# Attention's product of probabilities with values in full float32, each head on its own 64 columns of the array

## The chip, the cores and the metric

The kernel runs on one core of one Trainium2 chip. The metric is the device time of one execution in microseconds; times of several executions are given by their median. Its engines are TensorE (PE; the loading of a stationary operand is shown as PEld), VectorE (DVE), ScalarE (ACT), GpSimd (POOL) and SyncE (SP).

## The reference

A trunk of two layers on x of shape 1 x 256 x 1024, all in float32. Layer 0 is FFN, mLSTM mixer, FFN; layer 1 is FFN, windowed attention, FFN. After each of the six stages x becomes LayerNorm(alpha * x + stage(x)). The stage that the change touches is the attention of layer 1: 16 query heads of size 64, 4 key and value heads (four query heads share one), 256 tokens, a window of 128 to both sides, an ALiBi bias and a sink logit per head.

```python
s = jnp.einsum('bnqkgd,bnskd->bnkgqs', q, kw).astype(jnp.float32) * (HEAD_DIM ** -0.5)
s = jnp.where(valid, s - slopes * dist, MASK_VALUE)
m = jnp.maximum(jnp.max(s, axis=-1, keepdims=True), sink_l)
pe = jnp.exp(s - m)
attn = pe / (jnp.sum(pe, axis=-1, keepdims=True) + jnp.exp(sink_l - m))
o = jnp.einsum('bnkgqs,bnskd->bnqkgd', attn, vw.astype(jnp.float32)).reshape(B, S, nq)
return o.astype(x.dtype) @ w_out
```

The change is about the last einsum, attention's probabilities times values.

## The kernel before

**Products in three terms.** Nearly all products run on operands of type float32r, split in two: a high part (a copy by ACT into float32r) and a low part (the original minus the high part, by DVE). `mm3` (L617) issues three matmuls, high by high, high by low and low by high. The weights, 206 MB of reads over the execution, are loaded by SP and POOL queues into `w_raw` and `s_raw` buffers, split on ACT (`w_hi`) and DVE (`w_lo`) in `high` and `low` of the class `Weights`, and multiplied.

**Order of the work.** Each engine works through its instructions in the order in which the program issues them. The class `Paced` wraps the engines and keeps a clock for each; `on_tensor` (L162) adds a cost for every matmul. In the FFN stages `W.fill` reads these clocks after every matmul and decides which split comes next on ACT and DVE. In the attention stage there is no filler (L1600): `W.done` issues a counted number of splits, from the lists at the head of the file (`PU` for the attention loop), whatever the clocks say.

**The attention stage** (`attn`, L1335). `proj` multiplies x with the columns for keys and values and for the first queries. Its evacuation for m = 0 splits the values into `va[t]`, one tile per block of 128 tokens, of shape 128 x 4 x 5 x 64: for each of the four value heads there are five slots of 64 columns, of which slots 1 and 3 hold the high and the low part and slots 0, 2 and 4 are zeros, filled by POOL (L1371). A window of 128 columns that starts at slot 0 or 1 has the values in its right or left half and zeros in the other half.

Then a loop over `st` from 0 to 10 (L1552) treats heads in eight pairs j, software-pipelined: at step st it does, in this order,

- `values(st - 3)` and the evacuation of its sum into `qT` (high on ACT, low on DVE; rows `q_hi<-pw`, `q_lo<-pw`);
- the rest of the softmax of pair st - 1: `es` on ACT, the sum and its reciprocal `sm` and four scalings of `sc` on POOL (`scale`);
- some of the filling work in `fill[st]`: `q_rest` (remaining query columns) in early steps, `out_part` (the output projection of finished pairs) in later ones;
- `turn(st - 2, 0)`: four transposes of `sc` into a PSUM bank and a copy on ACT into `pr`;
- `W.done`: weight splits, on ACT at once;
- `scores(st)`: twelve matmuls, each head of the pair with 64 rows of the array of its own and a PSUM bank of its own; four fused reductions on DVE (bias, mask and row maximum `nm`); between them `flush(1)`; then `turn(st - 2, 1)`; then the exponentials on ACT;
- `flush(2)`: the rest of the pending low parts; then low parts of weights, and the rest of the filling work.

`turn` puts the low part of the probabilities (PSUM minus high part) on a list, and `flush` issues it on DVE. So in the kernel before, each pair has two such subtractions of 128 x 512, one per key block sb.

`values(j)` makes one PSUM bank of 128 x 256: head a of the pair in partitions 64a to 64a + 63. It issues twelve matmuls, all with 128 columns of `va` as stationary operand and 256 columns of `pr` moving: per key block, high values by high probabilities, low values by high probabilities, high values by low probabilities, and each of these for both heads. The zeros in the stationary operand make head 0 add nothing to the partitions of head 1 and the reverse.

After the loop `tail` does the remaining output projection and the LayerNorm, and the last FFN follows.

In the trace all tensor, vector and scalar instructions have the line of the recording helper, L180; they are told apart by the names of their tiles. `pw` and `py` are the two sets of four PSUM banks.

Of the kernel before, what the change touches and what calls it, by code (L numbers as in the profile page):

```python
# [9 lines left out]
F32 = mybir.dt.float32  # L10
FR = mybir.dt.float32r
# [15 lines left out]
TAGS = ("w_raw", "s_raw0", "s_raw1", "s_raw2", "s_raw3")  # L27
# [37 lines left out]
class Paced:  # L65
# [94 lines left out]
            self.mark(o, self.act + 125)  # L160

    def on_tensor(self, name, n, out, ins):  # L162
        self.pe = max(self.pe, self.when(*ins)) + (109.0 if name == "transpose" else n / 2.4 + 13.3)
        for o in out:
            self.mark(o, self.pe + 200)
        if self.filler is not None:
            self.filler()
# [21 lines left out]
class Weights:  # L189
# [134 lines left out]
    def low(self):  # L324

        nc = self.nc
        i, hi = self.half.pop(0)
        p = self.plan[i]
        k, scale, raw = p["k"], p["scale"], self.raw[p["word"]]
        lo = self.pool.tile([128, D], FR, name="w_lo", tag="w_lo", bufs=RING)  # L330
        if i == 0:
            for j in range(2):
                s_ = slice(j * 512, j * 512 + 512)
                nc.vector.tensor_sub(lo[:, s_], raw[:, s_], hi[:, s_].bitcast(F32))
        elif scale is None:
            nc.vector.tensor_sub(lo, raw, hi.bitcast(F32))
        else:
            nc.vector.scalar_tensor_tensor(lo, raw, scale(), hi.bitcast(F32), op0=OP.mult, op1=OP.subtract)
        self.parts[i] = (hi.rearrange("p (k f) -> p k f", k=k), lo.rearrange("p (k f) -> p k f", k=k))
        self.fresh = i  # L340
        sums = [(i, *sum_) for sum_ in self.after.get(i, ())]
        while sums and not isinstance(sums[0][2], int):
            self.transfer(*sums.pop(0)[1:])
        self.sums += sums
        self.drop(p["word"])
        self.load()
# [98 lines left out]
def trunk_kernel(ctx: ExitStack, tc: tile.TileContext, x, ffn_w_in, ffn_w_out, ln_g, ln_b, ml_w_in, ml_gate_b,  # L445
                 ml_norm_g, ml_w_out, at_w_in, at_sink, at_w_out, out):
    nc = Paced(tc.nc)
# [135 lines left out]
    W = Weights(nc, wpool, rooms, words, plan, after)  # L583
# [33 lines left out]
    def mm3(o, l, r, start, stop, onto=False):  # L617
        nc.tensor.matmul(o, l[0], r[0], start=start, stop=False, skip_group_check=onto)
        nc.tensor.matmul(o, l[0], r[1], start=False, stop=False, skip_group_check=onto)
        nc.tensor.matmul(o, l[1], r[0], start=False, stop=stop, skip_group_check=onto)  # L620

    def pair(p, *idx):
        return p[0][idx], p[1][idx]

    def wbank(shape=(128, 512)):
        return psum.tile(list(shape), F32, name="pw", tag="pw", bufs=4)
# [6 lines left out]
    def tok(t):  # L633
        return slice(t * 128, (t + 1) * 128)

    def split_evac(dst, src, scale=None, high=None, wait=False):
        if scale is None:
            (high or nc.scalar.copy)(dst[0], src)
            low = lambda: nc.vector.tensor_sub(dst[1], src, dst[0].bitcast(F32))
            if wait:  # L640
                W.when_ready(low, dst[0])
            else:
                low()
        else:
            nc.scalar.activation(dst[0], src, AF.Copy, scale=scale)
            nc.vector.scalar_tensor_tensor(dst[1], src, scale, dst[0].bitcast(F32), op0=OP.mult, op1=OP.subtract)
# [688 lines left out]
    def attn(l, n, pending, last):  # L1335
        with ExitStack() as ph:
            pool = ph.enter_context(tc.tile_pool(name="attn", bufs=1))
            tile_ = lambda shape, dt, name, **kw: pool.tile(shape, dt, name=name, tag=kw.pop("tag", name), **kw)

            def both(shape, name, bufs=1):  # L1340
                return tuple(tile_(shape, FR, name + e, bufs=bufs) for e in ("_hi", "_lo"))
# [24 lines left out]
                                        base=128, channel_multiplier=-sign)  # L1366
            dist = tile_([128, 2, S], F32, "dist")
            nc.gpsimd.tensor_add(dist, fwd, back)
            va = [tile_([128, 4, 5, 64], FR, f"v{t}") for t in range(2)]
            for t in range(2):  # L1370
                nc.gpsimd.memset(va[t][:, :, 0:5:2].bitcast(F32), 0.0)  # L1371
            qT = both([128, 8, S], "q")
            kd, qd = [], []

# [2 lines left out]
            def proj(t, m):  # L1377
                ps = wbank()
                for k in range(8):
                    if t == 0 and m == 1 and k == PEND[bound[0] - 1]:  # L1380
                        pending()
                        W.done(0, PD[bound[0] - 1])
                    if 4 * m + k // 2 == len(pieces):
                        pieces.extend(W.take(1))
                    mm3(ps, pair(xT, A, k, tok(t)), pair(pieces[4 * m + k // 2], A, k % 2), k == 0, k == 7)
                    if t == 1 and k % 2:
                        W.done(W.used - 8 + 4 * m + k // 2 + 1, 1 if m == 0 and k < 4 else 0)
                if m == 0:
                    kv = ps.rearrange("p (a g d) -> p a g d", a=2, g=4)
                    kk = tile_([128, 4, 2, 64], F32, "kd", tag="sc", bufs=6)  # L1390
                    nc.scalar.copy(kk, kv[:, 0, :, None, :].to_broadcast([128, 4, 2, 64]))
                    split_evac((va[t][:, :, 1], va[t][:, :, 3]), kv[:, 1])
                    kd.append(kk)
                else:
                    qq = tile_([128, 4, 128], F32, "qd", tag="sc", bufs=6)
                    nc.vector.tensor_mul(qq.rearrange("p j (a d) -> p (j a) d", a=2),
                                         ps.rearrange("p (h d) -> p h d", h=8),
                                         qs_row[:, :, None].to_broadcast([128, 8, 64]))
                    qd.append(qq)
# [27 lines left out]
            sc, pr = {}, {}  # L1427
# [64 lines left out]
            def turn(j, sb, p):  # L1492
                for t in range(2):
                    for a in range(2):
                        nc.tensor.transpose(p[:, a, tok(t)], sc[j, t][:, a, tok(sb)], ident)
                r = W.room(f"pr{sb}", TAGS[2 + sb]).bitcast(FR).rearrange("p (e a s) -> p e a s", e=2, a=2)
                d = (r[:, 0], r[:, 1])
                nc.scalar.copy(d[0], p)
                lows.append((d, p))
                pr[j, sb] = d  # L1500

            lows, sums = [], {}

            def values(j):
                p = wbank((128, S))
                terms = [(sb, a, e, f) for sb in range(2) for e, f in ((0, 0), (1, 0), (0, 1)) for a in range(2)]
                for n_, (sb, a, e, f) in enumerate(terms):
                    v = va[sb][:, j // 2].rearrange("p s d -> p (s d)")
                    at = 128 * e + 64 * (1 - a)
                    nc.tensor.matmul(p, v[:, at:at + 128], pr[j, sb][f][:, a], start=n_ == 0, stop=n_ == len(terms) - 1)  # L1510
                sums[j] = p
                for sb in range(2):
                    del pr[j, sb]
                    W.back(TAGS[2 + sb], 1)
# [17 lines left out]
            def parts(f_, *args):  # L1532
# [3 lines left out]
                return [lambda t=t, o=o: out_part(args[0], t, o) for t in args[1] for o in range(2)]  # L1536

            proj(0, 0)
            proj(0, 1)
            nc.scalar.preload_act_table(AF.Exp)  # L1540
            proj(1, 0)
            k_turn(0)
            q_turn(0)
# [8 lines left out]
            for st in range(11):  # L1552
                if st == 2:
                    gb = load_ln(lambda name: tile_([128, D], F32, name), l, n)
                if 0 <= st - 3 < 8:
                    values(st - 3)
                    o = sums.pop(st - 3)
                    d = pair(qT, A, st - 3)
                    nc.scalar.copy(d[0], o)
                    nc.vector.tensor_sub(d[1], o, d[0].bitcast(F32))  # L1560
# [8 lines left out]
                if 0 <= st - 2 < 8:  # L1569
                    for f_ in work[:FB[st]]:  # L1570
                        f_()
                    work = work[FB[st]:]
                    p0, p1 = wbank((128, 2, S)), wbank((128, 2, S))
                    turn(st - 2, 0, p0)
                    late = lambda: turn(st - 2, 1, p1)
                    if st >= 8 or not SW:
                        late()
                        late = None
# [18 lines left out]
    for j, (kind, l, i, n) in enumerate(stages):  # L1597
        last = j == len(stages) - 1
        bound[0] = j
        nc.filler = W.fill if kind == "ffn" else None  # L1600
        if kind == "ffn":
            pending = ffn(l, i, n, pending, last)
        elif kind == "mlstm":
            pending = mlstm(l, n, pending, last)
        else:
            pending = attn(l, n, pending, last)
# [29 lines left out]
```

## Time and profile before

| | us |
|---|---|
| timed executions | 913.14, 914.07, 913.46 |
| median | 913.46 |
| profiled execution, first to last instruction | 911.7 |

The profiled execution's span, 911.7 us, is from the first to the last instruction; the timed median is 1.8 us longer, which lies around the span. Every time from the trace below counts from the span's start. The attention loop lies at about 669 to 718 us, the last FFN behind 740 us.

In the profile's rows, "x12" is the number of instructions merged or grouped. A row of the timeline gives start, duration, engine, line, operation, output and inputs, and shapes; of a matmul the shape of the stationary operand (128\*128, or 64\*128 where it has 64 rows) and of the moving one. Matmuls overlap in the array, and their ends are modelled, so the time that one costs is read from one start to the next. A note in brackets is idle time of the engine ahead of the row and what ended it. In a row of windows stand the stretch, then for PE, PEld, DVE, ACT and POOL the busy time and the count, then the granted clock, the DMA share and GB/s. A row of groups ends with busy time and mean ns of one, and then the idle time ahead of the group.

### The profile page before, as it was taken

Reading aid. Unit: us, or ns where it says so; the run is one execution under the profiler, and the core shown is the slowest. Engines: PE = TensorE matmul, PEld = TensorE weight load, DVE = VectorE, ACT = ScalarE, POOL = GpSimd, SP = SyncE. Lnnn points to the kernel's source line nnn. Section 1 sums busy time; section 2 is a strip of 40 time slices with the busy share of each in tenths; the row PEclk is TensorE's granted clock in tenths of the full one; section 3 lists DMA queues with packets and bytes.
Section 4 is the critical chain, followed back from the end, with each engine's and each line's share of the span. In section 5 each row is a group of like instructions: output and inputs, shape, how many; then the busy total and the mean of one; then the engine's idle time right before and its main releaser. Section 6 shows DMA issues by size and latency. Waiting matters only on the chain.

```text
span 911.7 us, 12563 instructions
## 1 busy us (share of the span) xinstructions
PE 902.5 (99%) x4459; PEld 757.4 (83%) x4459; DVE 804.4 (88%) x971; ACT 573.1 (63%) x793; POOL 152.5 (17%) x192
## 2 busy tenths in 40 slices
PE   9999999999999999999999999999999999999996
PEld 7888888889988888888888888888898888888885
DVE  5999999886799898999888899998869889899886
ACT  5776777356664656776646676764569566676660
POOL 0111123113211011212011111110425301111110
PEclk9999999999999999999999999999999999999999
DMA  8999998546637898997868989986534587899851
GB/s 281 367 328 259 288 274 215 162 137 186 208 111 246 296 234 244 290 285 234 241 193 269 259 257 283 272 223 197 159 119 140 163 293 221 204 298 278 252 138 47
DMA packets 100703, 208.53 MB, mean 229 GB/s; under 512 B 6904, under 2 KB 21264, under 8 KB 100640
## 3 DMA queue, kind: packets, MB, share of 16 engines
q1 hardware_dynamic: 82368, 173.04, 54.2%
q0 software_dynamic: 17696, 33.65, 22.3%
q10 hardware_dynamic: 576, 1.05, 0.3%
q8 instruction: 35, 0.57, 0.3%
q14 instruction: 28, 0.23, 0.1%
HBM read 206.65 MB, written 1.05 MB: 228 GB/s over the span
## 4 chain that ended last, share of the span: by engine, by line
PE 98%; DVE 1%; DMA 0%; issue 0%; DVEq 0%
PE pw L180 64%; PE py L180 35%; DMA x<-in_x_dram 0%; DVE x L180 0%; DVE stats L180 0%; DVEq L1632 0%; DVE mv L180 0%; DVE rs L180 0%
## 5 line engine op out<-in xcount | busy, mean ns | idle before, releaser
L180 DVE TENSOR_TENSOR w_lo<-w_raw,w_hi 128x1024 fp32r<-128x1024 f32 (+1 forms) x213 | 255.2, 1219 | 26.6 <-ACT w_hi L180 24.8
L180 ACT CAST w_hi<-w_raw 128x1024 fp32r<-128x1024 f32 (+1 forms) x213 | 218.9, 1049 | 80.3 <-PE py L180 21.7
L180 DVE TENSOR_TENSOR w_lo<-s_raw,w_hi 128x1024 fp32r<-128x1024 f32 x192 | 228.6, 1219 | 18.3 <-ACT w_hi L180 18.2
L180 ACT CAST w_hi<-s_raw 128x1024 fp32r<-128x1024 f32 x192 | 196.6, 1054 | 58.4 <-PE py L180 23.3
L180 PE MATMUL pw<-w_hi,xT_hi 128*128 128x512 f32 x480 | 189.5, 396 | 0.0
L180 PE MATMUL pw<-w_hi,xT_lo 128*128 128x512 f32 x480 | 187.0, 391 | 0.0
L180 PE MATMUL pw<-w_lo,xT_hi 128*128 128x512 f32 x480 | 186.7, 390 | 0.0
L122 POOL DMA_DIRECT2D s_raw<-in_ffn_w_in_dram x64 | 77.4, 1211 | 484.1 <-DVE s_raw L180 226.3
L180 PE MATMUL py<-w_hi,h_hi 128*128 128x512 f32 x349 | 138.2, 396 | 0.0
L180 PE MATMUL py<-w_hi,h_lo 128*128 128x512 f32 x349 | 136.2, 390 | 0.0
L180 PE MATMUL py<-w_lo,h_hi 128*128 128x512 f32 x349 | 136.0, 390 | 0.0
L180 PEld LDWEIGHTS pw<-w_hi,xT_lo 128*128 128x128 f32 x480 | 90.0, 188 | 19.1
L180 PEld LDWEIGHTS pw<-w_lo,xT_hi 128*128 128x128 f32 x480 | 90.3, 188 | 18.6 <-DVE w_lo L180 1.2
L180 PEld LDWEIGHTS pw<-w_hi,xT_hi 128*128 128x128 f32 x480 | 90.1, 188 | 17.4 <-ACT w_hi L180 0.2
L180 PE MATMUL pw<-w_hi,S_hi 128*128 128x512 f32 x256 | 99.7, 390 | 0.0
L180 PE MATMUL pw<-w_lo,S_hi 128*128 128x512 f32 x256 | 99.7, 389 | 0.0
L180 PE MATMUL pw<-w_hi,S_lo 128*128 128x512 f32 x256 | 99.7, 389 | 0.0
L180 PEld LDWEIGHTS py<-w_hi,h_lo 128*128 128x128 f32 x349 | 65.5, 188 | 14.1
L180 DVE TENSOR_TENSOR s_raw<-s_raw,s_raw 128x1024 f32<-128x1024 f32 x64 | 76.8, 1219 | 0.3
L180 PEld LDWEIGHTS py<-w_lo,h_hi 128*128 128x128 f32 x349 | 65.7, 188 | 13.0
L180 PEld LDWEIGHTS py<-w_hi,h_hi 128*128 128x128 f32 x349 | 65.6, 188 | 12.7
L180 PEld LDWEIGHTS pw<-w_hi,S_lo 128*128 128x128 f32 x256 | 48.1, 188 | 10.0
(205 smaller groups left out, 1122.7 us busy)
## 6 DMA issues: line engine op xcount, KB each, us to landing
s_raw<-in_ffn_w_in_dram SPq DMA_DIRECT2D x96, 512.0 KB, 8.0
w_raw<-in_ffn_w_out_dram SPq DMA_DIRECT2D x88, 512.0 KB, 6.1
w_raw<-in_ffn_w_in_dram SPq DMA_DIRECT2D x64, 512.0 KB, 5.7
s_raw<-in_ffn_w_in_dram POOLq DMA_DIRECT2D x64, 512.0 KB, 8.3
w_raw<-in_ml_w_in_dram SPq DMA_DIRECT2D x24, 512.0 KB, 4.6
w_raw<-in_ffn_w_in_dram SPq DMA_DIRECT2D x32, 256.0 KB, 6.0
w_raw<-in_at_w_in_dram SPq DMA_DIRECT2D x12, 512.0 KB, 4.8
w_raw<-in_ml_w_out_dram SPq DMA_DIRECT2D x8, 512.0 KB, 4.1
```

What stands on the lines that cost most here:

```text
L122: self.nc.gpsimd.dma_start(ap, source, accum_op=OP.add)
L180: r = f(out, *args, **kw)
```

## The change

Values are kept once, as plain float32 of 128 x 4 x 64 per token block, copied by ACT; the zero slots, their fills and the split of the values go. The probabilities are copied once, as float32, into the first half of the same buffer; their low parts go, so that the list `lows` stays empty and `flush` issues nothing. `values` issues four matmuls instead of twelve: for each key block, head 0 into partitions 0 to 63 of the bank and head 1 into partitions 64 to 127, each with the 64 value columns as stationary operand and 256 moving columns, all in float32. The planner's `on_tensor` charges a float32 matmul twice the time per column; `values` has the only such matmuls.

```diff
     def on_tensor(self, name, n, out, ins):
-        self.pe = max(self.pe, self.when(*ins)) + (109.0 if name == "transpose" else n / 2.4 + 13.3)
+        passes = 2.0 if name == "matmul" and ins[0].dtype == F32 else 1.0
+        self.pe = max(self.pe, self.when(*ins)) + (109.0 if name == "transpose" else passes * n / 2.4 + 13.3)
...
-            va = [tile_([128, 4, 5, 64], FR, f"v{t}") for t in range(2)]
-            for t in range(2):
-                nc.gpsimd.memset(va[t][:, :, 0:5:2].bitcast(F32), 0.0)
+            va = [tile_([128, 4, 64], F32, f"v{t}") for t in range(2)]
...
-                    split_evac((va[t][:, :, 1], va[t][:, :, 3]), kv[:, 1])
+                    nc.scalar.copy(va[t], kv[:, 1])
...
-                r = W.room(f"pr{sb}", TAGS[2 + sb]).bitcast(FR).rearrange("p (e a s) -> p e a s", e=2, a=2)
-                d = (r[:, 0], r[:, 1])
-                nc.scalar.copy(d[0], p)
-                lows.append((d, p))
-                pr[j, sb] = d
+                r = W.room(f"pr{sb}", TAGS[2 + sb]).rearrange("p (e a s) -> p e a s", e=2, a=2)
+                nc.scalar.copy(r[:, 0], p)
+                pr[j, sb] = r[:, 0]
...
             def values(j):
                 p = wbank((128, S))
-                terms = [(sb, a, e, f) for sb in range(2) for e, f in ((0, 0), (1, 0), (0, 1)) for a in range(2)]
-                for n_, (sb, a, e, f) in enumerate(terms):
-                    v = va[sb][:, j // 2].rearrange("p s d -> p (s d)")
-                    at = 128 * e + 64 * (1 - a)
-                    nc.tensor.matmul(p, v[:, at:at + 128], pr[j, sb][f][:, a], start=n_ == 0, stop=n_ == len(terms) - 1)
+                for sb in range(2):
+                    for a in range(2):
+                        nc.tensor.matmul(p[64 * a:64 * a + 64], va[sb][:, j // 2], pr[j, sb][:, a],
+                                         start=sb == 0, stop=sb == 1)
```

## The prediction

> **What bounds the kernel now.** I read the page first: the share of each engine, the granted clock and the chain that ended last.
>
> ```profile
> span 911.7 us, 12563 instructions
> PE 902.5 (99%) x4459; PEld 757.4 (83%) x4459; DVE 804.4 (88%) x971; ACT 573.1 (63%) x793; POOL 152.5 (17%) x192
> ...
> PEclk9999999999999999999999999999999999999999
> ...
> PE 98%; DVE 1%; DMA 0%; issue 0%; DVEq 0%
> ```
>
> TensorE is busy for 99% of the span at full clock, and the chain that ended last runs through it for 98%. Time that the change takes from TensorE's queue, or puts there, therefore arrives at the end unless another engine stops TensorE instead. The change lies in the attention loop alone, so I next read the windows of that loop (PE, PEld, DVE, ACT, POOL, with counts) and the last FFN, which follows it.
>
> ```profile
> 676.00:689.40 13.40, 13.40 (x112) 12.14 (x112) 11.02 (x30) 13.19 (x42) 7.01 (x14) 1.00 0.51 158
> 689.40:708.50 19.10, 19.10 (x147) 16.33 (x145) 17.16 (x46) 17.32 (x49) 10.99 (x22) 1.00 0.51 155
> 708.50:718.00 9.50, 9.50 (x67) 8.57 (x66) 6.40 (x13) 6.08 (x18) 4.28 (x9) 1.00 0.42 133
> 740.00:911.70 171.70, 164.67 (x757) 136.48 (x755) 149.77 (x164) 100.41 (x121) 21.17 (x18) 0.99 0.74 212
> ```
>
> In the attention loop ACT, with 63% over the span, is nearly full: idle for 13.40 - 13.19 = 0.21 us in the first stretch and for 19.10 - 17.32 = 1.78 us in the second, 1.99 us together. That is the second limit here: however short TensorE's part becomes, these 32.5 us cannot shrink by more than about 1.99 us while ACT's work stays the same. In the third stretch, which has no scores and no exponentials, ACT has 3.42 us to spare.
>
> **What the changed part costs today.** The tile views of the transposed probabilities and of the values, and the timeline of TensorE with each block of `values` and the row that follows it (start, duration; the modelled duration overlaps the next row, so I go from start to start):
>
> ```profile
> L180 PE MATMUL pw<-pr,v x96: 278/283/390, 681.1 to 717.6; 128*128 128x256 f32 x96
> ...
> L180 DVE TENSOR_TENSOR pr<-pw,pr x16: 679/686/692, 679.7 to 716.5; 128x512 fp32r<-128x512 f32 x16
> ```
>
> ```profile
> L1371 POOL MEMSET v<- x2: 737/737/737, 657.3 to 657.9; 128x768 f32 x2
> ```
>
> ```profile
> 681.10 1.60 PE L180 MATMUL pw<-pr,v 128*128 128x256 f32 x12
> 682.54 0.60 PE L180 MATMUL pw<-ident,sc 128*128 128x128 f32 x4
> ...
> 685.96 1.94 PE L180 MATMUL pw<-pr,v 128*128 128x256 f32 x12
> 687.74 0.40 PE L180 MATMUL py<-w_hi,q_hi 128*128 128x512 f32 x1
> ...
> 692.45 1.80 PE L180 MATMUL pw<-pr,v 128*128 128x256 f32 x12
> 694.09 0.60 PE L180 MATMUL pw<-ident,sc 128*128 128x128 f32 x4
> ...
> 698.76 1.59 PE L180 MATMUL pw<-pr,v 128*128 128x256 f32 x12
> 700.19 0.60 PE L180 MATMUL pw<-ident,sc 128*128 128x128 f32 x4
> ...
> 703.50 1.80 PE L180 MATMUL pw<-pr,v 128*128 128x256 f32 x12
> 705.14 0.60 PE L180 MATMUL pw<-ident,sc 128*128 128x128 f32 x4
> ...
> 708.47 1.80 PE L180 MATMUL pw<-pr,v 128*128 128x256 f32 x12
> 710.11 0.39 PE L180 MATMUL py<-w_hi,q_hi 128*128 128x512 f32 x1
> 710.34 0.40 PE L180 MATMUL py<-w_lo,q_hi 128*128 128x512 f32 x1
> ...
> 712.37 1.71 PE L180 MATMUL pw<-pr,v 128*128 128x256 f32 x12
> 713.92 0.40 PE L180 MATMUL py<-w_hi,q_hi 128*128 128x512 f32 x1
> ...
> 716.19 1.70 PE L180 MATMUL pw<-pr,v 128*128 128x256 f32 x12
> 717.73 0.40 PE L180 MATMUL py<-w_hi,q_hi 128*128 128x512 f32 x1
> ```
>
> The eight blocks take 1.44, 1.78, 1.64, 1.43, 1.64, 1.64, 1.55 and 1.54 us: 9.57 for the first six, 3.09 for the last two, 12.66 in all, 1.58 on average. An undisturbed block is 1.44 us, so one product with 256 columns costs 0.12 us; 12.66 - 8 x 1.44 = 1.14 us is waiting inside the blocks, mostly for the low part of the probabilities (DVE, 686 ns), which the last two products of a block need.
>
> **Part by part.** (1) Removed: twelve products per block, 12.66 us of TensorE's queue. (2) Added: four full float32 products per block, each of 256 columns on a stationary tile of 64 columns. No float32 product other than a transpose is in this trace, so I bound it. Below: it costs one pass like the float32r product, 0.12 us, and the two heads' products run side by side. Above: it costs four passes, because the kernel's own split shows what an exact product consists of: three of the four partial products of high and low parts are what `mm3` and `values` issue now, and the fourth is low by low. Four passes over 256 columns are two times 512 columns, and a product of 512 columns steps by 0.23 us (710.11 to 710.34), so 0.46 us per float32 product. I take the upper price, since exactness has to be paid for in this array, which today needs three passes for less. The Trainium skill, "FP8 and Floating Point Precision", TensorE Precision Notes, says the same: true FP32 takes four passes, the three here and low by low; no run here shows it yet.
>
> (3) Are the two heads' products concurrent? The scores of this same loop answer that for the other direction: each head has 64 rows of the array of its own.
>
> ```profile
> 700.72 0.39 PE L180 MATMUL pw<-kT_hi,q_hi 64*128 64x256 f32 x2
> 700.94 0.28 PE L180 MATMUL pw<-kT_lo,q_hi 64*128 64x256 f32 x2
> 701.06 0.28 PE L180 MATMUL pw<-kT_hi,q_lo 64*128 64x256 f32 x2
> ...
> 701.42 0.28 PE L180 MATMUL pw<-kT_hi,q_lo 64*128 64x256 f32 x2
> 701.63 0.66 PE L180 MATMUL pw<-ident,sc 128*128 128x128 f32 x4
> 702.04 0.47 PE L180 MATMUL py<-w_hi,q_hi 128*128 128x512 f32 x1
> 702.35 0.39 PE L180 MATMUL py<-w_lo,q_hi 128*128 128x512 f32 x1
> ...
> 710.80 1.03 PE L180 MATMUL pw<-ident,sc 128*128 128x128 f32 x8
> ...
> 711.91 0.40 PE L180 MATMUL py<-w_lo,q_hi 128*128 128x512 f32 x1
> ```
>
> A pair (x2) steps by 0.12 us, as much as one product alone: the halves run at the same time. I take the same for columns: two pairs, 2 x 0.46 = 0.92 us.
>
> (4) Changing the shape of the array costs something, and the same rows price it. A transpose away from the scores steps by 0.11 us: eight of them and a wide product of 0.23 take 1.11 (710.80 to 711.91). The four transposes ahead of the scores (700.19 to 700.72) take 0.53, so +0.09; the first pair takes 0.22 instead of 0.12, +0.10; the last pair 0.21, +0.09; and four transposes with the first wide product behind it 0.72 (701.63 to 702.35) instead of 0.67, +0.05. That is 0.33 us per block. In `values` the +0.10 should lie beside a first product that is longer than 0.22, so I take 0.23. The Trainium skill, "TensorEngine Tiling (Array Packing)", Key Properties, states the rule that speaks against this change: a change of tiling mode drains the array. By it the scores' 0.33 us is owed twice per turn of the loop; the rows agree with the rule, and without it a block would be 0.92 us.
>
> A new block is thus 0.92 + 0.23 = 1.15 us.
>
> (5) Removed on DVE: 16 subtractions of 686 ns (11.0 us) and two for the values. They are not on TensorE's chain apart from the 1.14 us above, but the first one of each turn (`flush(1)`, L1459) stands between the score reductions for which ACT waits:
>
> ```profile
> 704.18 0.51 ACT L180 ACTIVATE sc<-sc,nm 128x256 f32<-128x256 f32 x1 [0.63 <-DVE nm L180]
> ```
>
> That is where part of ACT's 1.99 us idle time sits, and the change lets ACT use it. (6) The copies on ACT stay, with the same sizes, so ACT gains nothing else. Two fills on POOL (2 x 0.74 us at 657) go; they lie beside the projection, whose products keep TensorE busy, and without that cover they would be worth 1.5 us. No DMA, queue or wait is added; the second copy of the probabilities is now wanted after two products instead of after six, so a block that starts ahead of that copy has less of its own to cover it; that cannot cost more than it did, since the low part that six products covered came after the same copy. PSUM banks come free one subtraction earlier, a gain that no wait of TensorE's asks for.
>
> (7) The kernel's planner charges a block 4 x 226.6 ns (2 x 256 / 2.4 + 13.3) where it charged 12 x 120, and no subtractions, so its clocks enter the last FFN 4.3 us (TensorE) lower than before. Inside attention the order is by counts, not by clocks, so only the last FFN can be reordered.
>
> **The sum.** First six blocks: 9.57 - 6 x 1.15 = 2.67 us less on TensorE, but ACT allows 1.99. Last two, where ACT has room: 3.09 - 2 x 1.15 = 0.79. Together 2.78 us off the profiled span of 911.7, 908.9. The median of the runs shown, 913.46, lies 1.8 us above that span; with the same surplus the forecast is 913.46 - 2.78 = 910.7 us.
>
> **Rivals.** A change of 0.2% is 1.8 us, about the least that a measurement tells from none here.
>
> *Half overlap.* If a float32 product is worked off as two loads of the stationary tile (high, then low) in the order written, the queue holds head 0 high, head 0 low, head 1 high, head 1 low. Started in order, only neighbours of different heads overlap: five steps of 0.23 instead of four. A block is 1.15 + 0.23 = 1.38, and the saving 12.66 - 8 x 1.38 = 1.62 us: 911.8. For it: the starts of the scores' products ascend strictly, and two heads alternate there after every single product. Against it: I see no row of such a double load.
>
> *Serial: slower.* If 64-column products of full float32 don't overlap at all (also the case in which the change doesn't do what it says), a block is 8 x 0.23 + 0.23 = 2.07, and eight of them are 16.56 against 12.66: 3.9 us more, 917.4. It decides from a block of 1.58 us upward, that is from six steps of 0.23 one behind the other. Against it: rows of the scores, where halves of the array do overlap; but those are halves by rows, with two PSUM banks, and these are halves by columns in one bank.
>
> *Replanned FFN.* The blocks shrink as forecast, but the last FFN takes its splits in another order and one piece comes late: one high and one low part on the chain,
>
> ```profile
> L180 DVE TENSOR_TENSOR w_lo<-w_raw,w_hi 128x1024 fp32r<-128x1024 f32 (+1 forms) x213 | 255.2, 1219 | 26.6 <-ACT w_hi L180 24.8
> L180 ACT CAST w_hi<-w_raw 128x1024 fp32r<-128x1024 f32 (+1 forms) x213 | 218.9, 1049 | 80.3 <-PE py L180 21.7
> ```
>
> 1.22 + 1.05 = 2.3 us, which leaves 0.5 of the gain: 913.0. Against it: DVE and ACT have over 20 us and 70 us to spare in that FFN's 171.7.
>
> **The numbers.** Forecast 0.42, half overlap 0.25, serial 0.20, replanned or otherwise eaten up 0.13. The forecast is faster by more than 0.2%; half overlap (0.18%) and most of the fourth case fall within it; serial is slower. Faster 0.42 + 0.04, same 0.25 + 0.05, slower 0.20 + 0.04. The lower end takes one pass per product: a block of 2 x 0.12 + 0.23 = 0.47, 1.99 from the first six and 3.09 - 0.94 = 2.15 from the last two, 4.1 us, 909.3. The upper end is serial, 917.4: with it left out, and the bad part of the fourth case, over 2 in 10 would be missing. The forecast's own range is 909.3 to 911.5: the upper end takes the whole 0.33 (a block of 1.25 and a saving of 1.99 + 0.59) and the 0.6 us by which the runs shown scatter upward (913.46 to 914.07).
>
> **What would show it.** In the changed profile: blocks whose start lies 1.15 us ahead of what follows, with head 0 and head 1 starting within a few ns (forecast), every second product starting alone (half overlap), or none overlapping (serial); ACT without idle time from 676 to 706; no row in which TensorE waits for a subtraction of `pr`; the last FFN as long as before (from the loop's end to the span's end, within 0.3 us). It is wrong if the block isn't near 1.2 us, or if the loop gets shorter and the end doesn't.

## The result and the profile after

The changed kernel takes 911.46 us (median of 8, 910.72 to 912.02) against 913.34 (median of 8, 912.82 to 915.18): 1.88 us or 0.2% less. The ratio to before is 0.9976, with a 95% interval of 0.9967 to 0.9985. A second series gave 911.29 against 913.65, ratio 0.9974 (0.9965 to 0.9983). Forecast were 910.7 us and a saving of 2.78. The direction is as forecast, and 911.46 lies in the forecast's own range of 909.3 to 911.5, at its upper end; 0.4 to 0.9 us of the saving is missing.

The page of the changed kernel, the same lines as before (span, busy times, the chain that ended last):

```profile
span 909.0 us, 12471 instructions
PE 900.0 (99%) x4427; PEld 748.9 (82%) x4427; DVE 794.7 (87%) x953; ACT 574.7 (63%) x793; POOL 159.0 (17%) x190
...
PE 97%; DVE 1%; POOL 0%; ACT 0%; issue 0%; DVEq 0%; POOLq 0%
```

DVE has 18 instructions fewer and is busy 9.7 us less. POOL has two instructions fewer (the fills, 1.5 us) and is busy 6.5 us **more**, although its work in the loop wasn't touched. POOL and ACT also appear on the chain that ended last, which was TensorE alone but for the ends. That is the odd line in this page, and the missing gain is behind it.

The windows of the loop and of the last FFN (PE, PEld, DVE, ACT, POOL):

```profile
676.00:689.40 13.40, 13.22 (x110) 10.36 (x110) 9.25 (x24) 13.37 (x41) 9.88 (x14) 1.00 0.51 182
689.40:708.50 19.10, 19.04 (x129) 12.99 (x130) 14.58 (x40) 18.45 (x54) 16.44 (x23) 1.00 0.47 139
708.50:718.00 9.50, 9.50 (x56) 6.77 (x55) 4.00 (x6) 6.57 (x12) 3.06 (x6) 1.00 0.41 121
```

POOL's extra time is here: 16.44 us in the middle stretch where it was 10.99, and DVE's 14.58 instead of 17.16. ACT is idle for 0.03 and 0.65 us instead of 0.21 and 1.78. In the second profile named below, whose loop begins as late as that of before, it is 0.21 and 0.68: the idle time that went, 1.1 us, went in the middle stretch.

The span of this profile is 2.7 us shorter than that of before, but not all of that is the change: at the first scores, ahead of the first changed product, it already leads by 1.00 us (668.05 against 669.05), and the second profile of the same kernel, taken for the experiments, doesn't (669.12). So I compare the loop alone, from the start of the first block of `values` to the start of the first product behind the last one. Timeline of TensorE, first, sixth and last block with the row behind each:

```profile
680.20 1.08 PE L181 MATMUL pw<-pr,v 128*64 128x256 f32 x8
681.22 1.27 PE L181 MATMUL pw<-ident,sc 128*128 128x128 f32 x4
...
706.72 1.08 PE L181 MATMUL pw<-pr,v 128*64 128x256 f32 x8
707.73 0.50 PE L181 MATMUL py<-w_hi,q_hi 128*128 128x512 f32 x1
...
713.77 1.08 PE L181 MATMUL pw<-pr,v 128*64 128x256 f32 x8
714.78 0.50 PE L181 MATMUL py<-w_hi,q_hi 128*128 128x512 f32 x1
```

Before, the loop took 717.73 - 681.10 = 36.63 us; now 714.78 - 680.20 = 34.58 (34.54 in the second profile). That is 2.05 us less, which agrees with the timed 1.9 to 2.4 us. The part up to the end of the sixth block went from 29.01 to 27.53 us (1.48 less, forecast 1.99), the rest from 7.62 to 7.05 (0.57 less, forecast 0.79). All eight blocks take 1.01 to 1.02 us and none waits inside. From the loop's end to the span's end it is 194.2 us against 193.9, and 194.0 in the second profile, and every engine issues the same instructions there in the same order as before.

The x8 says that each of the four float32 products is two instructions. Their starts in the first block, as the trace has them (us), with the last product ahead of the block and the first transpose behind it at the ends:

```
679.992 | 680.201 680.208  680.468 680.474  680.683 680.690  680.899 680.906 | 681.216 681.381
```

They come in pairs 7 ns apart: two instructions always run side by side, and a pair steps by 0.216 us. The step into the block is 0.209 where it was 0.120, the first pair steps by 0.267, the last by 0.317, and the first transpose by 0.165 where 0.109 would be undisturbed. The change of shape costs 0.09 + 0.05 + 0.10 + 0.06 = 0.30 us per block.

### The profile page after: what moved, and what is told of

It is laid out like the page before. It is cut to its first block, busy times and chain, and to the rows that moved or that the text cites. A ratio compares the mean times of both kernels' runs of the same rounds, so it can differ in the third digit from the quotient of the medians.

```text
span 909.0 us, 12471 instructions
## 1 busy us (share of the span) xinstructions
PE 900.0 (99%) x4427; PEld 748.9 (82%) x4427; DVE 794.7 (87%) x953; ACT 574.7 (63%) x793; POOL 159.0 (17%) x190
## 4 chain that ended last, share of the span: by engine, by line
PE 97%; DVE 1%; POOL 0%; ACT 0%; issue 0%; DVEq 0%; POOLq 0%
PE pw L181 63%; PE py L181 34%; DVE x L181 0%; DVE sc L181 0%; POOL sc L1488 0%; DVE w_lo L181 0%; ACT sc L181 0%; DVE stats L181 0%; POOL sm L1485 0%; DVEq L1628 0%; DVE q_lo L181 0%; ACT es L181 0%; ACT q_hi L181 0%; DVE sm L181 0%; DVE mv L181 0%
## 5 line engine op out<-in xcount | busy, mean ns | idle before, releaser
L181 PEld LDWEIGHTS pw<-w_hi,S_hi 128*128 128x128 f32 x256 | 48.1, 188 | 10.0
```

What stands on the lines that cost most here:

```text
L181: r = f(out, *args, **kw)
```

## The experiments

Two theories could explain why the loop gave 2.05 instead of 2.78 us. Theory P: the removed subtractions had kept DVE's low parts of the weights (`w_lo`) out of the way of POOL's scalings (`sc<-sc,sm`); without them the two collide, POOL is late and TensorE's transposes wait. Theory A, close to the forecast: ACT's work alone holds the loop. The first is suggested by the rows of POOL and DVE in one turn of the changed kernel (timelines of the two engines), by the loading of the transposed operand that follows, and by POOL's tile row over the whole loop:

```profile
701.85 1.32 DVE L181 TENSOR_TENSOR w_lo<-w_raw,w_hi 128x1024 fp32r<-128x1024 f32 x1
...
703.58 0.14 PEld L181 LDWEIGHTS pw<-ident,sc 128*128 128x128 f32 x1 [0.26 <-POOL sc L1488]
```

```profile
702.08 1.44 POOL L1488 TENSOR_SCALAR sc<-sc,sm 128x256 f32<-128x256 f32 x1
```

```profile
L1488 POOL TENSOR_SCALAR sc<-sc,sm x32: 478/483/2503, 674.0 to 711.8; 128x256 f32<-128x256 f32 x32
...
  POOL sc L1488: 1.7, 6
```

The scaling that starts at 702.08, while DVE is in a `w_lo`, takes 1.44 us instead of 0.48 and ends 0.35 us behind it, and the fourth transpose waits for it. Seven of the 32 scalings are stretched in this way (1.44 to 2.50 us), each beside a `w_lo`. In the kernel before none is, for there no scaling begins while a `w_lo` runs. Two `w_lo` begin during the last scaling of a turn; of these the first takes 1.53 us instead of 1.22, and the scaling stays short (POOL's tile row and that `w_lo`, before):

```profile
L1489 POOL TENSOR_SCALAR sc<-sc,sm x32: 477/478/482, 675.0 to 714.2; 128x256 f32<-128x256 f32 x32
...
681.67 1.53 DVE L180 TENSOR_TENSOR w_lo<-w_raw,w_hi 128x1024 fp32r<-128x1024 f32 x1
```

**The changed kernel again** (no edit).

> The changed kernel itself once more, for a second profile and as the measure for the runs beside it. From the first block of values to the first product behind the last block it took 34.6 us in its first profile (36.6 before). Both theories: 34.6 again within 0.2, ratio to before 0.998, and again about 7 of POOL's 32 scalings at 1.44 us or more instead of 0.48. The 1.0 us by which the first profile was ahead before the attention loop even began should not repeat; if it does, something outside the loop has changed.

Measured: 911.29 us, ratio 0.9974 (0.9965 to 0.9983); loop 34.54 us; the same seven scalings, to within 10 ns each (1.44 to 2.50 us); no lead ahead of the attention loop. The collision isn't chance: it repeats in each place.

**The subtractions back, as idle work.**

```diff
-                    nc.vector.tensor_sub(d[1], src, d[0].bitcast(F32))
+                    nc.vector.tensor_sub(d[1], src, d[0])
...
                 nc.scalar.copy(r[:, 0], p)
+                lows.append(((r[:, 0], r[:, 1]), p))
                 pr[j, sb] = r[:, 0]
```

> The 16 subtractions that the change took from DVE are put back as idle work (their result is read by nobody); the products stay as changed. Theory P (port): without these subtractions DVE reaches the low parts of the weights while POOL still scales the exponentials, POOL's scaling then waits for the whole DVE instruction, and TensorE's transposes wait for POOL. With them back, all 32 scalings take 0.48 us, TensorE waits for POOL nowhere, and the loop is no longer than 34.6 us although DVE does 11 us more (34.0 to 34.6, about 0.3 us faster or the same). Rival A (ACT): the loop is held by ACT alone, and POOL's long scalings lie in slack. Then the subtractions only delay the row maxima for which ACT waits, and the loop takes 35.2 to 36.0, about 1 us slower than the changed kernel.

Measured: 912.18 us, ratio 0.9984 (0.9975 to 0.9993); loop 717.05 - 682.03 = 35.02 us. Tile row of POOL's scalings, and the waits in the loop:

```profile
L1488 POOL TENSOR_SCALAR sc<-sc,sm x32: 473/478/482, 675.9 to 714.1; 128x256 f32<-128x256 f32 x32
```

```profile
ACT sc L181 <- DVE nm L181: 3.6, 5, 1.4
...
PEld pw L181 <- DVE q_lo L181: 1.9, 5, 0.5
```

Half and half. All scalings are short again, so it was the missing subtractions that brought the collision, as P says. But the loop is 0.4 us longer, not shorter: with the subtractions ACT waits 3.6 us for row maxima again (2.8 without), and the loads of TensorE wait 1.9 us for low parts of the queries (`q_lo`) that queue behind them on DVE. They also still wait 1.1 us for POOL (1.7 without), where P expected nothing. Neither range was met, since the edit moves two things in opposite directions. TensorE's steps, from one start to the next and added over the loop, tell them apart: the 56 transposes take 6.96 us instead of the changed kernel's 7.90, the last products of the scores 1.2 us more, because the transposes behind them wait for `q_lo`, and the blocks 0.2 us more.

**One wait more, ahead of the low parts of the weights.**

```diff
-                flush(2)
+                if W.half and 0 <= st - 1 < 8:
+                    nc.vector.tensor_copy(small("late", 2)[:, 0, 0:1], sc[st - 1, 1][:, 1, 0:1])
                 W.lows()
```

> Changed kernel with one wait more and nothing else: ahead of the low parts of the weights DVE copies one column of the last scaled block, so that it can't begin them before POOL is through with its four scalings. Theory P (POOL's scalings wait for whole low parts of weights on DVE, and TensorE's transposes for POOL): all 32 scalings take 0.48 us, TensorE's wait for POOL (1.7 us in the loop) goes, and the loop from the first block to the first product behind the last one takes 33.6 to 34.2 us instead of 34.6: a wait makes the kernel faster, by 0.4 to 1.0 us. Rival A (ACT holds the loop): a wait can only cost; 34.6 to 35.2.

`flush(2)` issues nothing in the changed kernel, so nothing is lost with it; `W.half` lists the weights whose low part is still due.

Measured: 910.95 us, ratio 0.9970 (0.9959 to 0.9980). Tile rows of the scalings and of the added copy, and the blocks (first, sixth and last):

```profile
L1488 POOL TENSOR_SCALAR sc<-sc,sm x32: 480/482/489, 676.0 to 713.0; 128x256 f32<-128x256 f32 x32
L181 DVE COPY late<-sc x6: 154/154/155, 683.2 to 709.0; 128x1 f32<-128x1 f32 x6
```

```profile
682.21 1.08 PE L181 MATMUL pw<-pr,v 128*64 128x256 f32 x8
683.22 0.66 PE L181 MATMUL pw<-ident,sc 128*128 128x128 f32 x4
...
708.04 1.08 PE L181 MATMUL pw<-pr,v 128*64 128x256 f32 x8
709.06 0.50 PE L181 MATMUL py<-w_hi,q_hi 128*128 128x512 f32 x1
...
715.01 1.08 PE L181 MATMUL pw<-pr,v 128*64 128x256 f32 x8
716.03 0.50 PE L181 MATMUL py<-w_hi,q_hi 128*128 128x512 f32 x1
```

The loop takes 716.03 - 682.21 = 33.82 us, 0.76 less than the changed kernel, though DVE now waits 6.8 us for POOL in it and has six instructions more. What the edit moves is the start of the low parts of the weights, and with it what follows them on DVE. This is theory P. TensorE's loads still wait 1.2 us for POOL in three places, but no transpose starts late for it any more.

The 0.76 us is a net figure. Added from start to start, the 56 transposes of the loop take 6.52 us instead of 7.90, so the collision had cost TensorE 1.4 us. The added wait gives 0.6 us of that back: it delays `q_lo` on DVE, and in the first turn the transposes behind the scores wait for it, 0.76 us from the start of the last scores to the first transpose where 0.21 is undisturbed.

```profile
685.27 0.66 PE L181 MATMUL pw<-ident,sc 128*128 128x128 f32 x4 [0.49 <-DVE q_lo L181]
```

Compared with before the loop is 2.81 us shorter, where the forecast had 2.78: 2.16 up to the end of the sixth block and 0.65 behind it. The whole kernel's time goes the same way, but its interval overlaps that of the changed kernel; the 0.76 us is read from the loop.

**Two of four scalings on DVE**, behind the score reductions.

```diff
-                for t in range(2):
-                    for a in range(2):
-                        nc.gpsimd.tensor_scalar(sc[j, t][:, a], sc[j, t][:, a], sm[:, t, a:a + 1], 1.0,
-                                                op0=OP.mult, op1=OP.mult)
+                for a in range(2):
+                    nc.gpsimd.tensor_scalar(sc[j, 0][:, a], sc[j, 0][:, a], sm[:, 0, a:a + 1], 1.0,
+                                            op0=OP.mult, op1=OP.mult)
+                for a in range(2):
+                    second.append((sc[j, 1][:, a], sm[:, 1, a:a + 1]))
...
-                flush(2)
+                while second:
+                    s_, m_ = second.pop(0)
+                    nc.vector.tensor_scalar(s_, s_, m_, None, op0=OP.mult)
                 W.lows()
```

> Changed kernel with two of the four scalings of each pair moved from POOL to DVE, issued behind the score reductions and ahead of the low parts of the weights. Theory P: POOL's two scalings end before DVE begins a low part, all of them take 0.48 us, the transposes no longer wait, and POOL's chain to the last transposes is about 0.9 us shorter: loop 33.2 to 34.0 us, 0.6 to 1.4 us faster than the changed kernel, about 910.5. Rival A: ACT holds the loop up to the last scores, only the end of the loop gains from the shorter chain on POOL: 34.2 to 34.6, at most 0.4 us faster.

Measured: 910.85 us, ratio 0.9970 (0.9960 to 0.9981), the lowest median of the study; beside it the changed kernel took 911.29. The loop takes 715.29 - 681.73 = 33.56 us, inside P's range and outside A's. Two of the 16 scalings left on POOL are a little stretched (0.60 and 0.63 us), beside scalings that DVE now does.

**The second copy of the probabilities on DVE instead of ACT.**

```diff
-                nc.scalar.copy(r[:, 0], p)
+                (nc.vector.tensor_copy if sb else nc.scalar.copy)(r[:, 0], p)
```

> Changed kernel with the second copy of the probabilities of each pair on DVE instead of ACT, behind the score reductions. ACT has 8 x 0.47 us less to do, DVE's low parts of the weights begin about 0.7 us later. Theory A: ACT held the loop, so it becomes 1 to 2 us shorter (32.6 to 33.6) and POOL's long scalings may stay. Theory P: it gains only as far as POOL's scalings become short again, 33.6 to 34.2, unless the second half of a block now waits for DVE's copy, which comes later than ACT's; then 34.6 or more.

Measured: 911.45 us, ratio 0.9978 (0.9968 to 0.9987); loop 715.95 - 681.48 = 34.47 us. ACT has the less to do that A counts on, and one scaling alone is stretched, but four of the eight blocks now wait inside (1.16 to 1.20 us), for DVE's copy:

```profile
PEld pw L181 <- DVE pr L181: 1.6, 4, 0.4
```

One wait replaced another, and 34.47 lies between P's two ranges. It speaks against A's 1 to 2 us and doesn't decide more.

**Both scalings and the first copy on DVE.** The kernel with two scalings on DVE, and:

```diff
-                nc.scalar.copy(r[:, 0], p)
+                (nc.scalar.copy if sb else nc.vector.tensor_copy)(r[:, 0], p)
```

> The kernel with two scalings on DVE (loop 33.56 us, ACT busy 19.04 of 19.10 us in the middle of the loop) with the first copy of the probabilities of each pair on DVE too, in the time in which DVE waits for the scores. Theory A (ACT is now the bound): ACT has 8 x 0.47 us less, the loop takes 32.4 to 33.2. Rival T (TensorE's own queue is the bound by now: before 36.63, of which the blocks' 4.5 us and some 1 us for the array's changes of shape give 33.2): 33.2 to 33.7, no change that can be measured.

Measured: 911.14 us, ratio 0.9975 (0.9964 to 0.9985); loop 715.03 - 681.59 = 33.44 us. The middle of the loop (window row; ACT is the fourth busy time), with two scalings on DVE and then with the copy there too:

```profile
689.40:708.50 19.10, 19.10 (x142) 13.44 (x141) 16.39 (x50) 19.04 (x56) 8.60 (x16) 1.00 0.51 161
```

```profile
689.40:708.50 19.10, 19.10 (x141) 13.57 (x141) 18.50 (x54) 17.14 (x52) 8.65 (x16) 1.00 0.54 165
```

ACT goes from 19.04 busy to 17.14, and the loop from 33.56 to 33.44; the timed ratios, 0.9970 and 0.9975, don't differ beyond their intervals. So an engine that is busy for 99.7% of a stretch held the loop by no more than 0.12 us. TensorE's own queue is the limit now: its steps in this run are as long as undisturbed ones but for one wait of 0.24 us (for `q_lo`, in the first turn), so about 33.2 of the 33.44 us are its own work, as rival T says. Theory A falls, and what is left to gain in this loop by moving work between engines is about 0.2 us.

**Products in another order**, both key blocks of one head and then of the other:

```diff
-                for sb in range(2):
-                    for a in range(2):
+                for a in range(2):
+                    for sb in range(2):
```

> Changed kernel with the four products of a block in another order: both key blocks of head 0, then both of head 1, so that neighbours in the queue use the same half of the array. Theory N (the halves overlap only where neighbours in the queue use different halves): no or one overlap, seven or eight streams of 0.21 us and the change of shape, 1.6 to 1.8 us per block instead of 1.01; loop about 38 to 40 us, 3.5 to 5 us slower than the changed kernel. Rival H (each half has a queue of its own): 1.01 as before, loop 34.6.

Measured: 911.65 us, ratio 0.9981 (0.9971 to 0.9990); loop 715.51 - 680.68 = 34.83 us. Blocks that have their data take 1.02 us, and the starts still come in pairs:

```
680.469 | 680.678 680.691  680.944 680.958  681.160 681.174  681.376 681.389 | 681.699 681.864
```

Now they lie 13 to 14 ns apart, with the same 0.216 between pairs. Three blocks take longer (1.17 to 1.24 us), and in them the pairs come apart into two rows. In the second block, counted from its first start (us):

```
0.000 0.266 0.482 0.698 | 0.230 0.496 0.712 0.928
```

One row keeps the undisturbed steps; the other begins 0.23 us late and then has the same steps. So a pair is one instruction of each head and not the two instructions of one product, each half of the array runs its products as they come, and neighbours in the program needn't use different halves (theory H). That one row begins late probably comes from the order: the second product now wants the second copy, and the other head's products stand behind it.

**Full float32 on all 128 columns**, with zeros beside the values as in the kernel before:

```diff
-            va = [tile_([128, 4, 64], F32, f"v{t}") for t in range(2)]
+            va = [tile_([128, 4, 3, 64], F32, f"v{t}") for t in range(2)]
+            for t in range(2):
+                nc.gpsimd.memset(va[t][:, :, 0:3:2], 0.0)
...
-                        nc.tensor.matmul(p[64 * a:64 * a + 64], va[sb][:, j // 2], pr[j, sb][:, a],
-                                         start=sb == 0, stop=sb == 1)
+                        v = va[sb][:, j // 2].rearrange("p s d -> p (s d)")
+                        nc.tensor.matmul(p, v[:, 64 * (1 - a):64 * (1 - a) + 128], pr[j, sb][:, a],
+                                         start=sb == a == 0, stop=sb == a == 1)
```

> Changed kernel, but each float32 product uses all 128 columns, with zeros beside the 64 value columns as in the kernel before: float32 without a half of the array for each head. If a full float32 product costs four passes whatever its columns, and the overlap of the two halves is what makes the change pay: eight streams of 0.21 to 0.23 us, 1.7 to 1.85 us per block, without the change of shape (about 0.15 us less around the block), loop 38 to 40 us, about 3 us slower than the kernel before. If the float32 product were cheaper than that (two passes), 0.85 to 0.95 per block and the loop shorter than 34.6.

Measured: 914.77 us, ratio 1.0009 (1.0000 to 1.0018): 0.9 us above before, and by the ratios about 3.1 us above the changed kernel. The loop takes 718.98 - 681.40 = 37.58 us, under the expected 38 to 40, and 0.95 us above before instead of about 3. First block:

```profile
681.40 1.89 PE L181 MATMUL pw<-pr,v 128*128 128x256 f32 x8
683.12 0.65 PE L181 MATMUL pw<-ident,sc 128*128 128x128 f32 x4
```

Eight instructions in 683.12 - 681.40 = 1.72 us, 0.215 each, and nothing overlaps: a product of 256 columns takes 0.43 us where one of float32r takes 0.12. Four blocks, those with transposes behind them, read so; the other four read 1.54, since the wide product behind them starts 0.19 us early and itself takes that much longer (0.42 instead of 0.23). Without the halves the float32 product costs more than the three terms it replaces, whose undisturbed block is 1.44 us.

## Why the prediction was right or wrong, point by point

**What bounds the kernel:** right. The time came out of TensorE's queue in the attention loop and arrived at the end; the last FFN is unchanged within 0.3 us.

**(2) A float32 product costs four passes:** the price is right, 0.43 us for 256 columns (0.46 forecast from the 512-column rows), 3.6 times the 0.12 us of a float32r product. The Trainium skill, "FP8 and Floating Point Precision", TensorE Precision Notes, says four passes; the trace agrees in the price and shows two instructions of 0.215 us, each nearly as long as a float32r product of 512 columns. It doesn't count passes.

**(3) The halves overlap by columns as they do by rows:** right, in pairs 7 ns apart. Half overlap and serial are both out. The half-overlap rival saw correctly that a product is worked off as two, but its reason for losing the overlap, a start in the order written, fails even when the heads don't alternate.

**(4) The change of shape:** 0.23 forecast, 0.30 measured, since 0.05 of the first pair's wait shows and the step out is 0.16 instead of 0.14. With the faster streams (4 x 0.216 = 0.86 instead of 0.92) a block costs 0.86 + 0.30 = 1.16 us with its surroundings; 1.15 was forecast.

**The sum:** the forecast 2.78 lies as near to the measured 2.05 as it does because two errors in it partly cancel, which is luck. TensorE's blocks alone give 12.66 - 8 x 1.16 = 3.4 us. The forecast cut this by a ceiling of 1.99 us on the first six blocks, taken from ACT's idle time; but with two scalings on DVE and all of ACT's copies in place these blocks take 26.6 us and save 2.4, and relieving ACT of 1.9 us in the middle stretch gave only 0.12 more in the whole loop. So the ceiling was too low by at least 0.4 us. Against that stands the collision, which takes 1.4 us and isn't in the sum: 3.4 - 1.4 = 2.0, and 2.05 was measured. That the loop with the added wait saves 2.81, nearly the forecast 2.78, is chance too: there 0.6 us is lost to the wait for `q_lo`.

**(5) The removed subtractions cost nothing:** this is the step that failed. The prediction took from DVE's queue 11 us of work that TensorE's chain hardly saw, found one gain in it (ACT's wait for row maxima) and priced what comes behind at nothing. What stands behind it in DVE's order is a low part of the weights of 1.22 us; it moved forward, so that it now runs when POOL wants to begin a scaling, which it never did in the kernel before. POOL's scalings grew by 8.0 us in all (32 of 0.48 before, seven of them 1.44 to 2.50 now); 1.4 us of that reached the transposes. The forecast of 2.78 in the loop became 2.05, and the timed saving 1.9 to 2.4.

**(7) The planner's clocks:** no instruction behind the loop changed its place. The rival of a replanned FFN is out.

**What would show it:** "ACT without idle time" was a bad sign to look for: ACT came close to it (18.45 of 19.10 us in the middle stretch) without being what held the loop.

## What to carry to other kernels

Taking work from an engine that isn't the limit still moves everything behind it forward; look at what comes next in that queue, and at which other engine it will then meet. A collision of DVE and POOL shows as the same instruction in two lengths: compare the minimum, median and maximum of a tile's rows before and after. And when an engine's busy share reads 99%, take some work off it before calling it the bound.

## What the runs showed of the hardware

A POOL instruction that reads SBUF and starts while DVE is in an instruction with two SBUF inputs waits until that one ends: 0.48 us became 1.44 to 1.52 beside one `w_lo` (1.25 to 1.49 us long), and 2.50 across two in a row, each time ending 0.26 to 0.35 us behind the `w_lo`. A `w_lo` that found POOL at work grew itself, from 1.22 to as much as 1.49 us (1.53 before). The Trainium skill, "SBUF — State Buffer", SBUF: two separate sides, calls this an exclusive lock held for the whole instruction; the lengths here agree. The subtractions that the change removed read one input from PSUM and one from SBUF, and no scaling beside them was stretched. Scalings on DVE, with one tensor input in SBUF, did stretch two on POOL, to 0.60 and 0.63 us.

Column halves of the array keep two queues of float32 products running whatever their order in the program (1.01 us alternating, 1.02 head by head, for blocks that have their data), and changing to them and back costs 0.30 us, as much as the row halves of the scores (0.33).
